# Fourier units between the halves of the output-gate units, folded weights cast one granule later, and a respaced folding stage in a one-core inference step

## The chip, the core and the metric

The kernel runs on one core of a Trainium2 chip. The metric is the time of the whole program in microseconds (us). Five engines work beside each other, each through its own list of instructions in order: TensorE (PE, the matmuls), VectorE (DVE), ScalarE (ACT), GpSimd (POOL) and SyncE (SP, which here only issues DMAs). Engines wait for each other through semaphores.

## The reference

One layer of a hybrid model on 384 tokens (128 context, 256 latent), model width 2048. The layer has a mixing sub-layer and a dense SwiGLU feed-forward; in each the input is normalised and modulated by six vectors of a per-layer map of the conditioning ("ada": `mod = silu(cond) @ w_ada + b_ada`). The change lies in the mixing sub-layer:

```python
proj = h @ w_in                       # GLA q, k, v, output gate g, decay factors, Fourier channels fo
o_f, s_f = gla_chunked(qh, kh, vh, la_f, s0_f, n_chunks)      # forward scan, la = log decay
o_b, s_b = gla_chunked(flip(qh), flip(kh), flip(vh), flip(la_b), s0_b, n_chunks)
o = rmsnorm_per_head(o_f + flip(o_b)) * gla_out_norm * silu(g)
f = fft2(fo.reshape(b, t, 4, 256), axes=(1, 3), norm='ortho').real
g_a, g_b = split(sigmoid(h @ w_gate + b_gate), 2)
merged = g_a * (o @ w_br_gla) + g_b * (f @ w_br_four)
return merged @ w_out, s_f, s_b
```

All values are float32.

## The kernel before

**Products in two parts.** Activations and weights are split into a rounded part (hi) and a remainder (lo), and a product is three matmuls: hi·hi, lo·hi, hi·lo. A weight granule is 128 x 1024 floats. SP loads it into `raw` (two buffers, in one stage up to two more); ACT casts it to `whi`; DVE subtracts to give `wlo`. `srcs` (from line 159) is the hand-written list of all granules in the order of use; `load` takes the next, `split` makes hi and lo, and `grab` returns the oldest finished pair and pushes one more through `load` and `split`. So each granule that PE begins to use emits, on SP, ACT and DVE, the work for granules that come later. `proj` is a product with the full 2048 rows: two granules, 24 matmuls each, into one PSUM tile `pmm`; what follows it (`dst`) is put in `later` and emitted after the first half of the next `proj`, or by `catch_up`.

**Order.** The order of instructions on PE, ACT, DVE and POOL is that of the code (a manual schedule); there is no planner. Side work is written as generators that are advanced one step per half of a `proj`; `paced` advances one by `rate[0]` steps a turn.

**Stages that the change touches.**

- GLA. Six q/k units and then 25 of the 32 gate units `h @ w_gate` run as `proj`, with the GLA heads as a side generator. Beside them a generator `ada` forms second-stage ada products: per step, POOL loads 512 KB of `w_ada` (`adaw`) and DVE adds it, weighted, to `adacc` (`ada_rest`, two instructions per step, 16 steps to a product), and at the end PE sums it over partitions with `selr` into `pr`; `ada_tail` copies this to `adev` (ACT), transposes it (`ptm`, PE) and writes `mods` (DVE). A gate unit ends on ACT with `gz` and a store of `gz` to DRAM (`gates_d`, line 962, by SP). In a head, ACT turns `z` into log decays `la` (lines 797 to 799), DVE makes the remainder `lal`, PE sums them to `bT`, and from this DVE makes `qi` and `ki`, with which PE forms `at` (line 854).
- Folding stage. The last seven gate units (14 half-units, "turns") run with `run_after` as their side work. Following the list `after` (lines 165 to 173) it folds h over mirrored positions, a pair of 128-row blocks at a time (`ends`: `t`, `r`; `over_parts`: `hF`), and multiplies the folded h by folded Fourier weights (`across_n`, eight steps for each of two halves of the channels, PSUM tiles `pfo`). The granules of `across_n` are unfolded in place by DVE (`fold_across`, lines 248 and 249). Here `raw` has two further buffers in another pool, named `raw3` in the order below.
- Output-gate stage (`mix_order`): eight units "o", each a `proj` of 48 matmuls ended by `gcol` (three transposes `pt`, the silu `gs` on ACT, `o_hi`), and after them Fourier units "b". `four` multiplies the spectrum by one granule of `w_br_four`, which `fold` first turns by DVE into sums and differences (`ws`, one buffer), copies out of PSUM (`fd`, ACT), assembles `y`, scales it by a gate (`gate`, sigmoid on ACT) and stores `y` to `four_d` in DRAM. Twelve of the sixteen "b" follow the "o" units 2 to 7, two each. A granule marked `hold` keeps its cast back until the unit's end (`settle`).
- The sixteen units "a" (`w_br_gla`) with the other four "b", then `w_out`. Another ada product, `summed` (`ada_gemv`), is formed on PE from `adaw` directly (`pr<-adaw,spad`) beside the "o" units.

```python
for b, i in mix_order:
    if b == "o":
        ...
        proj(psm, hT, lambda p, i=i: gcol(p, i), sd)
```

## Time and profile before

| | us |
|---|---|
| median of 3 runs | 1974.54 (1974.36 to 1977.55) |
| profiled execution, its own time | 1976.35 |
| its span in the trace | 1974.5 |
| PE busy | 1935.3 (98%) |
| DVE busy | 1637.8 (83%) |
| ACT busy | 914.5 (46%) |
| mean granted PE clock | 0.994 |

The stages in the trace, in us from the span's start: first modulation with the v and x products to about 145, GLA to 446, folding stage to 551, output-gate stage to 683, "a" units to 763, `w_out` to 905, a norm, and from 925 the feed-forward, whose order is the same in both kernels. A wait is an idle stretch of an engine put down to the instruction that released it; PE waits little, so each of its waits can be found by its place in these stages.

### The profile page before, as it was taken

How to read it: one execution, taken by the hardware profiler on the slowest of the kernel's cores; microseconds unless marked ns; L12 is line 12 of the kernel's file. 1: busy time of each engine (PE TensorE's matmuls, PEld its weight loads, DVE VectorE, ACT ScalarE, POOL GpSimd, SP SyncE). 2: the span in 40 equal slices, each digit the busy share in tenths (PEclk: the TensorE clock that was granted, in tenths of full speed). 3: DMA queues.
4: the chain of work that ended last, by engine and by line, in shares of the span. 5: the costliest groups of instructions: out<-in, count | busy, mean ns of one | idle time of the engine just before them, and what ended most of it. 6: DMA issues, size and time to landing. Idle time of an engine off the chain costs nothing.

```text
span 1974.5 us, 27637 instructions
## 1 busy us (share of the span) xinstructions
PE 1935.3 (98%) x10566; PEld 1699.0 (86%) x10566; DVE 1637.8 (83%) x2160; ACT 914.5 (46%) x1298; POOL 85.7 (4%) x154
## 2 busy tenths in 40 slices
PE   8998999999999899999999999999999999999997
PEld 5778999999988799999988888888888888888886
DVE  5668898888847688987789998999898989887885
ACT  4234445543555544446454444354444444444444
POOL 0000111110000000004000000000000000000001
PEclk9999999999999999999999999999999999999999
DMA  9976666775657787665335444453636263625243
GB/s 390 384 264 206 237 223 235 244 238 188 193 160 233 251 253 261 213 213 191 129 132 184 146 146 156 159 185 119 194 126 205 99 214 106 205 68 192 79 170 114
DMA packets 200616, 380.54 MB, mean 193 GB/s; under 512 B 14196, under 2 KB 126932, under 8 KB 196132
## 3 DMA queue, kind: packets, MB, share of 16 engines
q1 hardware_dynamic: 186004, 328.12, 48.9%
q0 software_dynamic: 13952, 50.39, 8.3%
q8 instruction: 83, 1.36, 0.3%
q14 instruction: 49, 0.40, 0.1%
q10 hardware_dynamic: 528, 0.26, 0.0%
HBM read 361.94 MB, written 16.78 MB: 192 GB/s over the span
## 4 chain that ended last, share of the span: by engine, by line
PE 80%; DVE 9%; DMA 5%; ACT 3%; issue 3%; SPq 0%; POOL 0%; DVEq 0%; ACTq 0%; POOLq 0%
PE pgu L327 30%; PE pmm L315 21%; PE pdn L327 17%; PE pv L477 3%; DVE adacc L679 2%; DVE wlo L276 1%; DMA raw<-in_w_in 1%; PE pgm L460 1%; PE pmm L1468 1%; PE pf L1205 1%; PE pfo L1017 1%; DMA slab<-in_w_ada 1%; PE ptr L1760 1%; DMA xraw<-in_w_x 1%; ACT whi L275 0%
## 5 line engine op out<-in xcount | busy, mean ns | idle before, releaser
L315 PE MATMUL pmm<-A_hi,whi 128*128 128x384 f32 x1072 | 364.9, 340 | 3.8 <-ACT gs L1167 3.8
L315 PE MATMUL pmm<-A_lo,whi 128*128 128x384 f32 x1072 | 360.9, 337 | 0.0
L315 PE MATMUL pmm<-A_hi,wlo 128*128 128x384 f32 x1072 | 360.4, 336 | 0.0
L1615 ACT CAST whi<-u 128x1024 fp32r<-128x1024 f32 x200 | 210.7, 1054 | 284.1 <-DVE u L1599 86.8
L1615 ACT CAST whi<-raw 128x1024 fp32r<-128x1024 f32 x175 | 184.1, 1052 | 197.8 <-PE pgu L327 59.9
L1626 DVE TENSOR_TENSOR wlo<-u,whi 128x1024 fp32r<-128x1024 f32 x200 | 244.5, 1222 | 32.9 <-ACT whi L1615 18.1
L275 ACT CAST whi<-raw 128x1024 fp32r<-128x1024 f32 x165 | 172.8, 1050 | 193.3 <-DMA raw<-in_w_gate 49.5
L276 DVE TENSOR_TENSOR wlo<-raw,whi 128x1024 fp32r<-128x1024 f32 x163 | 198.8, 1222 | 67.1 <-ACT whi L275 64.1
L327 PE MATMUL pgu<-whi,A_hi 128*128 128x512 f32 x640 | 250.1, 391 | 0.0
L327 PE MATMUL pgu<-whi,A_lo 128*128 128x512 f32 x640 | 249.3, 390 | 0.0
L1626 DVE TENSOR_TENSOR wlo<-raw,whi 128x1024 fp32r<-128x1024 f32 x175 | 213.8, 1222 | 36.0 <-ACT whi L1615 24.8
L315 PEld LDWEIGHTS pmm<-A_hi,whi 128*128 128x128 f32 x1072 | 202.8, 189 | 9.9 <-issue 4.5
L315 PEld LDWEIGHTS pmm<-A_lo,whi 128*128 128x128 f32 x1072 | 203.1, 189 | 0.6 <-DVE A_lo L365 0.5
L315 PEld LDWEIGHTS pmm<-A_hi,wlo 128*128 128x128 f32 x1072 | 202.8, 189 | 0.0
L679 DVE SCALAR_TENSOR_TENSOR adacc<-adaw,spad,adacc 128x1024 f32<-128x1024 f32 x150 | 185.8, 1281 | 1.6 <-DMA adaw<-in_w_ada 1.3
L327 PE MATMUL pdn<-whi,hid_hi 128*128 128x512 f32 x480 | 186.9, 389 | 0.0
L327 PE MATMUL pdn<-whi,hid_lo 128*128 128x512 f32 x480 | 186.8, 389 | 0.0
L327 PE MATMUL pgu<-wlo,A_hi 128*128 128x512 f32 x640 | 184.2, 389 | 0.0
L327 PEld LDWEIGHTS pgu<-whi,A_hi 128*128 128x128 f32 x640 | 120.2, 188 | 26.0 <-issue 0.8
L327 PEld LDWEIGHTS pgu<-wlo,A_hi 128*128 128x128 f32 x640 | 120.2, 188 | 25.3
L327 PEld LDWEIGHTS pgu<-whi,A_lo 128*128 128x128 f32 x640 | 120.2, 188 | 25.0
L327 PE MATMUL pgu<-whi,S 128*128 128x512 f32 x480 | 131.1, 395 | 0.0
(405 smaller groups left out, 3038.0 us busy)
## 6 DMA issues: line engine op xcount, KB each, us to landing
adaw<-in_w_ada POOLq DMA_DIRECT2D x96, 512.0 KB, 4.0
raw<-in_w_d SPq DMA_DIRECT2D x88, 512.0 KB, 3.8
slab<-in_w_ada SPq DMA_DIRECT2D x32, 1024.0 KB, 10.8
raw<-in_w_gate SPq DMA_DIRECT2D x64, 512.0 KB, 4.5
raw<-in_w_g SPq DMA_DIRECT2D x48, 512.0 KB, 3.3
raw<-in_w_u SPq DMA_DIRECT2D x48, 512.0 KB, 3.5
raw<-in_w_in SPq DMA_DIRECT2D x44, 512.0 KB, 4.3
u<-in_w_u SPq DMA_DIRECT2D x40, 512.0 KB, 4.6
```

The source lines that it names most:

```text
L275: ACT.copy(hi, raw)
L276: sub = lambda: eng.tensor_sub(lo, raw, hi.bitcast(F32))
L315: PE.matmul(dst, w[wi][:, k * n + n0 : k * n + n0 + P], x[xi][:, k0 + k, :], start=first and k == 0 and j == 0, stop=last and k == kts - 1 ...
L327: PE.matmul(dst, stat[x_][m], mov(w[w_], m), start=first and w_ == m == x_ == 0, stop=last and w_ == m == 1,)
L460: PE.matmul(pgv[q : q + 32, :], spad[:, k, :], slab[k // (KT // 2)][:, k % (KT // 2), :], start=k < 4, stop=k >= KT - 4,)
L477: PE.matmul(pv[2 * t + g], hT[x_][:, kb, t * P : (t + 1) * P], w_[:, g * 512 : (g + 1) * 512], start=kb == 0 and j == 0, stop=kb == KT - 1 ...
L679: DVE.scalar_tensor_tensor(acc[:, c, :], w, spad[:, k, c : c + 1], acc[:, c, :], op0=ALU.mult, op1=ALU.add,)
L1017: PE.matmul(p, w_of[0][:, i, k, g, :], x[:, :, lo:hi], start=kt == 0, stop=False)
L1205: PE.matmul(pf[:, 0 : 2 * HT], w[0][:, c], x[k], start=k == 0, stop=False)
L1468: PE.matmul(hp[u], hw[u][j][:, ((k - 1) % 8) * P : ((k - 1) % 8 + 1) * P], h2[m][:, k - 1, :], start=k == 1 and j == m == 0, stop=k == KT ...
L1615: ACT.copy(hi, src)
L1626: DVE.tensor_sub(lo, src, hi.bitcast(F32))
```

## The change

- Between the halves of the output-gate units 3 to 7 stands one Fourier unit, and one follows each of them; unit 2 is followed by one, and unit 7 by a second. `proj` gets `mid` for this. A unit in between with an odd number puts both of its PSUM tiles into the pool `pss`.
- The cast and the remainder of a folded granule are emitted at the next `split`, ahead of that granule's own; `hold` and `settle` are gone.
- `y` is kept in `unstored` and its store emitted a unit later.
- `summed` is advanced at the "a" units 0 and 3 (before 0 and 1), `ada` also at the "a" unit 5 and at turn 7 of the folding stage.
- Folding stage: the pairs get a free turn after the first four, the first `across_n` comes three turns after its `ends` (before two), and the second half of `across_n` goes into the last three turns.
- The last four steps of the fifth and last product of `ada_rest` run on PE (four matmuls each) in place of DVE; they fall among the half-units of `w_out`.
- `rate[0]` is 0.7 for the q/k units after the first (before 1.0), and 0.9 from `w_out` on (before 0.82).
- Gate units store `gz` from ACT's queue in place of SP's.

```diff
     for n in range(8):
-        after[n].append(("ends", n))
-        after[n + 1].insert(0, ("parts", n))
-        after[n + 2].insert(0, ("f", 0, n))
+        at = n + n // 4
+        after[at].append(("ends", n))
+        after[at + 1].insert(0, ("parts", n))
+        after[at + 3].insert(0, ("f", 0, n))
     for n in range(8):
-        after[10 + n * (turns - 10) // 8].append(("f", 1, n))
+        after[turns - 1 - (7 - n + 1) // 4].append(("f", 1, n))
...
-    mix_order = [("o", 0), ("o", 1)]
-    for i in range(2, 8):
-        mix_order += [("o", i)] + [("b", next(fourier)) for _ in range(BF * (i - 1) // 6 - BF * (i - 2) // 6)]
+    mix_order = []
+    between = [[] for _ in range(8)]
+    for i in range(8):
+        mix_order.append(("o", i))
+        if i > 2:
+            between[i].append(next(fourier))
+            mix_order.append(("b", between[i][0]))
+        mix_order += [("b", next(fourier)) for _ in range((i > 1) + (i == 7))]
...
         elif b == "b":
-            folded.add(len(srcs))
-            srcs.append(a["w_br_four"][i])
+            inner = any(i in x for x in between)
+            folded.add(len(srcs) - inner)
+            srcs.insert(len(srcs) - inner, a["w_br_four"][i])
...
+            for cast, _ in folded_due:
+                cast()
+            while folded_due:
+                folded_due.pop()[1]()
             if pairs == 1:
                 raw = fold(raw)
...
-            elif pairs and hold:
-                half_done.append(rest)
+            elif pairs:
+                folded_due.append((lambda: ACT.copy(hi, raw), low))
...
             step(side)
+            if not g:
+                for unit in mid:
+                    unit()
...
+            summed, pr = KT - 4 if (m, half) == todo[-1] else KT, None
             for k in range(KT):
                 w = adap.tile([P, 1024], F32, tag="adaw", name="adaw", bufs=2)
                 POOL.dma_start(w, a["w_ada"][m - 2, half, k])
+                if k >= summed:
...
+                    for j in range(4):
+                        PE.matmul(
+                            pr[32 * j : 32 * j + 32, :], spad[:, k, :], w[:, j * 256 : (j + 1) * 256],
+                            start=k == summed, stop=False,
+                        )
+                    yield
+                    continue
...
+        rate[0] = 0.7
         for i in qk_order[1:]:
             proj(psm, hT, keep(qk, i), sd)
+        rate[0] = 1.0
...
-                SP.dma_start(gates_d[i], g)
+                ACT.dma_start(gates_d[i], g)
...
-                if at == turns - 1:
+                if at in (7, turns - 1):
                     next(ada, None)
...
-            w = grab(hold=True)
             catch_up()
+            w = grab()
+            while unstored:
+                unstored.pop()()
...
-                pf = (pss if m else psm).tile([P, 512], F32, tag="side" if m else "mm", name="pf")
+                apart = m or i % 2
+                pf = (pss if apart else psm).tile([P, 512], F32, tag="side" if apart else "mm", name="pf")
...
-            SP.dma_start(four_d[i], y)
-            settle()
+            unstored.append(lambda: SP.dma_start(four_d[i], y))
+            gate_of()
...
-                proj(psm, hT, lambda p, i=i: gcol(p, i), sd)
+                proj(psm, hT, lambda p, i=i: gcol(p, i), sd, [lambda n=n: four(n) for n in between[i]])
...
-                if i < 2:
+                if i in (0, 3):
                     next(summed, None)
-                if KT - 7 <= i < KT - 2:
+                if i == 5 or KT - 7 <= i < KT - 2:
                     next(ada, None)
...
-        rate[0] = 0.82
+        rate[0] = 0.9
```

Where instructions stand now is shown at three places, before and then after; line numbers are those of each kernel. First ACT in the output-gate stage, one "o" unit with its two Fourier units. `gs` is the silu, `whi<-ws` the cast of folded Fourier weights, `whi<-raw` that of a granule of an "o" unit, `fd` the copy out of a Fourier unit's PSUM. Before:

```order
L1167 ACT_TABLE_LOAD
L1167 ACTIVATE gs<-pmm 128x384
L364 CAST o_hi<-gs 128x384
L1209 COPY fd<-pf 128x194 x2
L1192 ACT_TABLE_LOAD
L1192 ACTIVATE gate<-gate 128x384
L1209 COPY fd<-pf 128x194 x2
L275 CAST whi<-ws 128x1024
L1192 ACTIVATE gate<-gate 128x384
L275 CAST whi<-ws 128x1024
L275 CAST whi<-raw 128x1024 x2
```

After:

```order
L1194 ACT_TABLE_LOAD
L1194 ACTIVATE gs<-pmm 128x384
L376 CAST o_hi<-gs 128x384
L292 CAST whi<-ws 128x1024
L298 CAST whi<-raw 128x1024
L1239 COPY fd<-pf 128x194 x2
L1219 ACT_TABLE_LOAD
L1219 ACTIVATE gate<-gate 128x384
L292 CAST whi<-ws 128x1024
L298 CAST whi<-raw 128x1024
L1239 COPY fd<-pf 128x194 x2
L1219 ACTIVATE gate<-gate 128x384
```

The two casts of "o" granules, which stood together at the unit's end ahead of the next silu, stand apart, each behind the cast of a folded granule and ahead of a Fourier unit's copies.

Next DVE at the start of the folding stage. `raw3` with a fold (`128x2x256`) is the first granule of `across_n`; `hF` is what its matmuls read. Before:

```order
L248 TENSOR_TENSOR raw3_4518<-raw3_4518 128x2x256
L249 SCALAR_TENSOR_TENSOR raw3_4518<-raw3_4518 128x2x256
L709 TENSOR_TENSOR t_4556<-A_hi_92,A_lo_93 128x768
L714 TENSOR_TENSOR r_4557<-t_4556 128x2x64
L715 TENSOR_TENSOR r_4557<-t_4556 128x2x63
L714 TENSOR_TENSOR r_4557<-t_4556 128x2x128
L715 TENSOR_TENSOR r_4557<-t_4556 128x2x127
L282 TENSOR_TENSOR wlo_4530<-raw3_4518,whi_4529 128x1024
L276 TENSOR_TENSOR wlo_4569<-raw3_4520,whi_4568 128x1024
L721 TENSOR_TENSOR hF_4513<-r_4557,hF_4513 128x2x384
```

After:

```order
L285 TENSOR_TENSOR wlo_4511<-raw3_4502,whi_4510 128x1024
L734 TENSOR_TENSOR t_4538<-A_hi_92,A_lo_93 128x768
L739 TENSOR_TENSOR r_4539<-t_4538 128x2x64
L740 TENSOR_TENSOR r_4539<-t_4538 128x2x63
L739 TENSOR_TENSOR r_4539<-t_4538 128x2x128
L740 TENSOR_TENSOR r_4539<-t_4538 128x2x127
L254 TENSOR_TENSOR raw3_4504<-raw3_4504 128x2x256
L255 SCALAR_TENSOR_TENSOR raw3_4504<-raw3_4504 128x2x256
L746 TENSOR_TENSOR hF_4497<-r_4539,hF_4497 128x2x384
L734 TENSOR_TENSOR t_4580<-A_hi_92,A_lo_93 128x768
```

The gate granule now comes ahead of the first granule of `across_n` and goes first into the additional buffers; the first `hF` stands ahead of the remainder of the `across_n` weights.

Last ACT in a GLA head beside a gate unit. Before:

```order
L961 ACTIVATE gz<-pmm,bgate 128x384
L797 ACTIVATE la<-z 128x512
L797 ACTIVATE la<-z 128x256
L798 ACTIVATE la<-la 128x768
L799 ACT_TABLE_LOAD
L799 ACTIVATE la<-la 128x768
L364 CAST lah<-la 128x768
```

After:

```order
L988 ACTIVATE gz<-pmm,bgate 128x384
L989 DMA gates_d<-gz 128x384
L822 ACTIVATE la<-z 128x512
L822 ACTIVATE la<-z 128x256
L823 ACTIVATE la<-la 128x768
L824 ACT_TABLE_LOAD
L824 ACTIVATE la<-la 128x768
L376 CAST lah<-la 128x768
```

The store's issue stands between `gz` and the head's first step.

More of the change, by code (lines that the diff above doesn't have):

```diff
@@ L39 @@
 GF = 25
-BF = 12
 GD = 256
@@ L254, in fold_across, with split @@
         )
-    def split(at=None, eng=DVE, hold=False, defer=None):
+    def split(at=None, eng=DVE, defer=None):
         if raws:
@@ L270, in split, with low @@
             )
+            for cast, _ in folded_due:
+                cast()
+            while folded_due:
+                folded_due.pop()[1]()
             if pairs == 1:
                 raw = fold(raw)
[L274 to L277 removed]
+            def low():
+                eng.tensor_sub(lo, raw, hi.bitcast(F32))
                 ready.append((hi, lo))
@@ L281, in split, with push @@
                 ACT.copy(hi, raw)
-                low_due.append(lambda: (DVE.tensor_sub(lo, raw, hi.bitcast(F32)), ready.append((hi, lo))))
-            elif pairs and hold:
-                half_done.append(rest)
-            else:
-                rest()
-    def settle():
-        if half_done:
-            half_done.pop()()
-    def push(at=None, eng=DVE, hold=False):
+                low_due.append(low)
+            elif pairs:
+                folded_due.append((lambda: ACT.copy(hi, raw), low))
+            elif defer is not None:
+                ACT.copy(hi, raw)
+                defer.append(lambda: eng.tensor_sub(lo, raw, hi.bitcast(F32)))
+                ready.append((hi, lo))
+            else:
+                ACT.copy(hi, raw)
+                low()
+    def push():
         if not depth[0]:
@@ L683, in ada_rest @@
             yield
-            pr = pss.tile([P, 256], F32, tag="side", name="pr")
+            opened = pr is not None
+            if not opened:
+                pr = pss.tile([P, 256], F32, tag="side", name="pr")
             for c in range(2):
@@ L688, in ada_rest @@
                         pr[32 * j : 32 * j + 32, :], selr[:, 32 * c : 32 * c + 32],
-                        acc[:, c, j * 256 : (j + 1) * 256], start=c == 0, stop=c == 1,
+                        acc[:, c, j * 256 : (j + 1) * 256], start=c == 0 and not opened, stop=c == 1,
                     )
@@ L1232, in tile_step @@
             if b == "b":
-                for g in (df, nw):
-                    for _ in g:
-                        pass
-                four(i)
+                if not i:
+                    for g in (df, nw):
+                        for _ in g:
+                            pass
+                if not any(i in x for x in between):
+                    four(i)
             else:
```

25 lines of the change are left out of this document (13 added, 12 removed).

## The prediction, made before the changed kernel ran

> **What bounds the kernel now.** First the page, to see which engine is full; then TensorE's (PE's) waits, because a full engine loses time only where it waits; then stretches of equal work and the timeline, to see what each wait costs.
>
> ```profile
> span 1974.5 us, 27637 instructions
> PE 1935.3 (98%) x10566; PEld 1699.0 (86%) x10566; DVE 1637.8 (83%) x2160; ACT 914.5 (46%) x1298; POOL 85.7 (4%) x154
> ```
>
> PE is busy for 98% of the span. An edit that leaves PE's matmuls alone can only win back PE's waits and the slow clock behind them. PE's waits, longest in total first (us, times, longest):
>
> ```profile
> PE pmm L315 <- ACT gs L1167: 5.8, 4, 2.3
> PE at L854 <- DVE ki L831: 4.6, 1, 4.6
> ...
> PE pfo L1017 <- DVE hF L721: 4.2, 1, 4.2
> PE ptm L657 <- ACT adev L653: 2.8, 2, 2.3
> ...
> PE pr L687 <- DVE adacc L679: 1.1, 2, 0.6
> ...
> PE bT L814 <- DVE lal L365: 0.7, 1, 0.7
> ```
>
> All of these lie where the change works. What a wait drags behind it is read from the granted clock of the 3.5 us after five of them (start and end of a stretch, its length, busy time of PE, PEld, DVE, ACT and POOL with their instructions, then the clock, the DMA share and GB/s):
>
> ```profile
> 689.60:693.00 3.40, 3.40 (x12) 3.40 (x13) 3.37 (x7) 1.30 (x2) 0.00 (x0) 0.54 0.84 286
> 682.85:686.30 3.45, 3.45 (x20) 3.45 (x21) 2.80 (x9) 2.79 (x6) 0.00 (x0) 1.00 0.94 344
> 463.10:466.60 3.50, 3.50 (x16) 3.50 (x17) 3.43 (x8) 1.29 (x4) 0.00 (x0) 0.63 0.64 208
> 648.00:651.50 3.50, 3.50 (x14) 3.50 (x13) 2.86 (x10) 3.16 (x7) 0.00 (x0) 0.55 0.54 150
> 877.40:880.90 3.50, 3.50 (x13) 3.50 (x13) 2.98 (x8) 0.33 (x1) 0.00 (x0) 0.57 0.96 327
> ```
>
> Behind the 2.3 (ptm) the clock was 0.54, behind the 4.2 (pfo) 0.63, behind the 2.3 (pmm at 647.68) 0.55, behind the three short ones at 874 to 877 0.57; behind the pmm wait that ended at 682.85 it stayed 1.00. (At full clock 20 matmuls took 3.45: 0.17 each.) So such a stretch costs 3.4 x 0.46 = 1.6, 3.5 x 0.37 = 1.3, 3.5 x 0.45 = 1.6 and 3.5 x 0.43 = 1.5 us more.
>
> **The change part by part.**
>
> *Fourier units between the halves.* Four stretches of the output-gate stage, from one unit's wait to the next; each holds one output-gate unit and two Fourier units, in the same columns:
>
> ```profile
> 614.45:629.50 15.05, 15.05 (x103) 13.64 (x101) 11.16 (x23) 8.07 (x11) 1.05 (x2) 1.00 0.74 253
> 629.50:647.68 18.18, 15.42 (x103) 13.72 (x101) 12.15 (x26) 10.05 (x16) 1.05 (x2) 1.00 0.67 220
> 647.68:665.51 17.83, 16.82 (x101) 15.26 (x101) 12.12 (x25) 9.49 (x14) 1.06 (x2) 0.90 0.71 222
> 665.51:682.85 17.34, 15.28 (x101) 13.72 (x101) 12.12 (x25) 9.49 (x14) 1.05 (x2) 1.00 0.76 247
> ```
>
> The first had no wait and took 15.05 for the same matmuls. Why the others wait is on the timeline:
>
> ```profile
> 639.41 0.33 SPq L227 DMA_DIRECT2D raw<-in_w_in  x1
> 644.78 1.05 ACT L275 CAST whi<-raw 128x1024 fp32r<-128x1024 f32 x1 [3.31 <-DMA raw<-in_w_in]
> 647.14 0.49 ACT L1167 ACTIVATE gs<-pmm 128x384 f32<-128x384 f32 x1
> 647.68 0.44 PE L315 MATMUL pmm<-A_hi,whi 128*128 128x384 f32 x1 [2.28 <-ACT gs L1167]
> ```
>
> ACT stands in order. A cast whose weights were still in flight (issued 639.41, cast 644.78: 5.37) stood ahead of the silu (with its table load between, from the cast's end at 645.83 to 647.14), and the silu frees the PSUM tile that PE's next unit writes. The change puts a Fourier unit between the two halves, so that the silu of the last unit now stands ahead of these casts on ACT, and the folded cast is emitted at the next granule's split. PE's matmuls per unit are as many as before; DVE has 12.15 and ACT 10.05 of work for 15.05 of PE, so neither is full. With every unit at 15.05: 18.18 + 17.83 + 17.34 - 3 x 15.05 = **-8.2**. The other end is -5, if one unit in three keeps its wait. I take -8.2, since a unit of that length stands in the trace. The y stores, a unit later on SP, stand behind weight loads that are needed sooner; the first reader is an "a" unit several units on: nothing.
>
> *summed.* The tail of the second-stage ada product was: copy at the first "a" unit, transposes at the next, PE waiting 2.3 for the copy. The transposes now come three units later, when the copy has long run: -2.3 and the slow stretch of 1.6, **-3.9** (to -2.3 if the stretch comes back elsewhere).
>
> *Folding stage.* Rows from its start:
>
> ```profile
> 451.73 0.38 SPq L227 DMA_DIRECT2D raw<-in_w_in  x1
> 455.48 0.69 DVE L248 TENSOR_TENSOR raw<-raw 128x512 f32<-128x512 f32 x1 [4.13 <-DMA raw<-in_w_in]
> 456.82 0.95 DVE L709 TENSOR_TENSOR t<-A_hi,A_lo 128x768 f32<-128x768 f32 x1
> 458.88 1.22 DVE L282 TENSOR_TENSOR wlo<-raw,whi 128x1024 fp32r<-128x1024 f32 x1
> 463.11 0.42 PE L1017 MATMUL pfo<-hF,whi 128*128 128x388 f32 x1 [4.20 <-DVE hF L721]
> ```
>
> PE came to its first across unit at 463.11 - 4.20 = 458.91 and waited for DVE, which had waited 4.13 for a load that could go only at 451.73. Now one more half gate unit lies ahead, 24 matmuls of 0.17, 4.1: PE comes at 463.0. DVE now runs, from the landing near 455.5: cast and remainder of the gate granule (1.05 + 1.22), one fold of a pair up to its remainder step (458.88 - 456.82 = 2.06), the unfolding of the weights (456.82 - 455.48 = 1.34), hF (0.95), another 2.06 and the remainder of the across weights (1.22): 455.5 + 9.9 = 465.4, less some overlap of neighbouring instructions (0.1 each, about 0.4). So 465.0, and with PE coming between 463.0 and 463.1 the wait is about 1.9 in place of 4.2, -2.3; and as the wait before 682.85, 17.34 - 15.28 = 2.06, left the clock whole, the slow 1.3 goes as well: **-3.6**. Bounds: -5.5 (both all gone) and -1 (the bunched across units of the last turns wait for weights).
>
> *Fewer ada steps at the start (rate 0.7).*
>
> ```profile
> 178.89 3.86 SPq L227 DMA_DIRECT2D raw<-in_w_in  x2
> 184.74 1.05 ACT L275 CAST whi<-raw 128x1024 fp32r<-128x1024 f32 x1 [8.12 <-DMA raw<-in_w_in]
> 193.94 0.59 PE L854 MATMUL at<-qi,ki 128*64 128x64 f32 x12 [4.57 <-DVE ki L831]
> ...
> raw<-in_w_in SPq DMA_DIRECT2D x44, 512.0 KB, 4.3
> ```
>
> Two ada steps of DVE fewer stand ahead of ki, but the chain to it starts at a cast that waited for a DMA, not for DVE. That load, the first of the pair issued from 178.89 on, took 5.8 where such loads land in 4.3 (median); with two fewer 512 KB ada loads beside it I give it 4.3: **-1.4**. Bounds: 0 (it stays 5.8) and -5.9 (the wait of 4.57 gone with its slow clock). The 0.9 in w_out meets no wait of PE there: nothing.
>
> *Last ada product partly on PE.*
>
> ```profile
> 603.45 0.34 PE L315 MATMUL pmm<-A_hi,wlo 128*128 128x384 f32 x1
> 603.72 0.64 PE L700 MATMUL pr<-adaw,spad 128*32 128x256 f32 x8
> 604.57 0.34 PE L315 MATMUL pmm<-A_lo,whi 128*128 128x384 f32 x1
> 876.84 0.56 PE L657 MATMUL ptm<-ident,adev 128*128 128x128 f32 x2 [0.49 <-ACT adev L653]
> ```
>
> Four steps move from DVE to PE. One such step between matmuls takes 604.57 - 603.45 - 2 x 0.17 = 0.78, so four cost **+3.1**. In return the two waits for adacc go (**-1.1**), and with them I take half of the slow 1.5 (**-0.8**): the 0.49 for adev stays.
>
> *Gate stores on ACT.* A store now stands on ACT between gz and la:
>
> ```profile
> 244.94 0.57 ACT L961 ACTIVATE gz<-pmm,bgate 128x384 f32<-128x384 f32 x1
> 245.41 0.86 ACT L797 ACTIVATE la<-z 128x512 f32<-128x512 f32 x2
> 251.33 0.96 DVE L365 TENSOR_TENSOR lal<-la,lah 128x768 fp32r<-128x768 f32 x1 [0.96 <-ACT lah L364]
> 252.70 0.27 PE L814 MATMUL bT<-cg,lal 128*128 128x128 f32 x1
> 1965.71 0.42 ACTq L1916 DMA_DIRECT2D out_yT<-x1b  x1
> gates_d<-gz SPq DMA_DIRECT2D x32, 192.0 KB, 3.7
> ```
>
> It waits for gz's end (245.51) and takes 0.42 (ACT's only other DMA kind), so la starts about 0.65 later. lal ended 0.4 ahead of bT here, and in another head PE already waited 0.7 for it: 0.25 + 0.65 + about 0.1 for the three heads that have such a chain, **+1.0** (0 to +2.1). The other stores lie beside an ACT that is busy 46%. The Trainium skill's page "DMA: Bandwidth & Descriptors", section "Issuing engines are not separate DMA queues", says that issuing from a second engine saves only the issuing sequencer's time; by that the move wins nothing but SP's issue, and no term here counts a gain for it.
>
> Sum: -8.2 - 3.9 - 3.6 - 1.4 + 3.1 - 1.1 - 0.8 + 1.0 = **-14.9**. The profiled execution took 1976.35, span 1974.5; it would take 1961.4. The median is 1974.54: forecast **1959.6**.
>
> **The rivals.**
>
> *Only the waits of the mixing stage go.* The folding stage and the start keep theirs, since both begin with a load that starts no sooner. -8.2 - 3.9 - 1.9 + 3.1 + 1.0 = -9.9: 1964.6. For it: both chains start at a DMA. Against: the folding stage gets 4.2 of PE work ahead of the wait.
>
> *The slow clock is not the waits' doing.* The Trainium skill's page "TensorE: Matmul & The Clock Gate", section "Part 1: The HAM clock gate", ties half speed to an idle window of about 3.4 us, free-running; the trace disagrees, with 0.54 and 0.55 behind waits of 2.3. As a mechanism of this kernel: if those stretches come by their own rhythm, the 1.6 of ptm, the 1.6 in the mixing stage and the 0.8 stay, +4.0: 1963.6.
>
> *ACT is held until its store lands.* Were it held for the 3.7 of the store's row, la would start 3.8 later in three heads: 3.4 + 3.8 + 3.4 = 10.6, each with a slow stretch of about 1.5, less the 1.0 counted: +14.1, so 1973.7. It decides once ACT's delay passes 0.65 by far. Against: the row of 0.42 is the issue alone.
>
> *Two raw buffers bound each Fourier unit (slower).* A unit of four granules over two raw buffers takes two rounds of load to cast 5.37, cast 1.05, remainder 1.22 and what its steps stand in a queue. With no queueing that is 15.3, hardly over the 15.05. If the folded cast, a granule later, puts two steps of about 0.95 more into each round, 1.9, a unit is 2 x 9.54 = 19.1, and with a slow stretch of 1.5 it is 20.6. The stage has about four such units of (15.05 + 18.18 + 17.83 + 17.34) / 4 = 17.1: +14 in place of -8.2, 1981.8. It turns slower once a unit passes some 19 us. For it: three of four stretches were 17.3 to 18.2, and their wait began at a load. Against: one ran at 15.05 on the same two buffers, and the late cast was read from ws, a buffer of its own.
>
> **How the numbers follow.** Forecast 0.60, waits of the mixing stage alone 0.15, clock rhythm 0.05, ACT held 0.08, two buffers 0.12. A measurement of this kernel can tell about 0.2%, 3.9 us, so faster is below 1970.6 and slower above 1978.5: faster 0.60 + 0.15 + 0.05 = 0.80, same 0.08, slower 0.12. The range leaves out the last two: its high end, 1969, has the bounds at -5 for the units, -2.3 for summed, 0 at the start and little in the folding stage; its low end, 1951, has the waits at the start and in the folding stage gone (-4.5 and -1.9 more) and the store free.
>
> **What would show it.** In the profile after: no wait of pmm for gs, stretches of about 15 us per output-gate unit at clock 1.00; no ptm wait near 690; a pfo wait of about 2 near 465; at waiting about 3 near 192; no wait for adacc near 875; bT waiting in two or three heads for under 1. A cast waiting for raw in the Fourier units, with PE waiting for wlo or whi behind it, would make the forecast wrong; so would la following its store by 3 us or more.

## The result, and the profile after

The changed kernel takes 1977.63 us (median of 19 runs, 1975.27 to 1981.23), the kernel before 1974.11 (19 runs): ratio 1.0022, 95% interval [1.0015, 1.0029]. It is slower by about 0.2%, where 0.8% faster was forecast. Its profiled execution took 1977.9, 1.5 over the 1976.35 of before. The medians stand 3.5 apart, so the profiles below account for the 1.5 only.

The top of the page after: PE is as full as before.

```profile
span 1976.0 us, 27636 instructions
...
PE 1937.8 (98%) x10598; PEld 1698.8 (86%) x10598; DVE 1628.8 (82%) x2152; ACT 916.4 (46%) x1298; POOL 86.1 (4%) x154
```

PE's waits after (us in total, times, longest): the four waits of pmm for gs are gone. Those of pfo, the across units of the folding stage, come six times and add up to 7.6 (before three times and 4.7). And pmm now waits for gate, a DVE step of the a units.

```profile
PE at L879 <- DVE ki L856: 4.8, 2, 4.6
...
PE pfo L1045 <- DVE wlo L285: 3.7, 3, 2.3
PE pmm L324 <- DVE gate L1285: 3.3, 2, 2.8
PE pfo L1044 <- ACT whi L289: 3.2, 2, 2.4
...
PE z L814 <- ACT krs L802: 1.7, 1, 1.7
PE ptm L669 <- ACT adev L665: 1.0, 1, 1.0
PE pfo L1044 <- DVE X L1052: 0.7, 1, 0.7
```

`X` is the sum of the first channel half, which DVE adds up from pfo before PE can write the second half into it.

The stages tell more than the waits. These are stretches of the same work, cut at landmarks on PE: folding stage (last po to first pfq), output-gate stage (first pt to first matmul on o), a units to the last Fourier unit, the six a units behind it, w_out (which after holds the last ada product's matmuls too, 838 for 806). Columns as in the prediction. Before:

```profile
437.79:548.63 110.84, 106.17 (x644) 105.07 (x642) 92.00 (x135) 50.57 (x84) 5.32 (x10) 0.98 0.60 190
569.65:682.85 113.20, 107.37 (x705) 95.60 (x703) 74.10 (x143) 61.20 (x93) 7.39 (x14) 0.98 0.67 214
682.85:738.35 55.50, 53.20 (x309) 52.88 (x310) 48.69 (x93) 30.18 (x53) 0.53 (x1) 0.97 0.83 262
738.35:763.27 24.92, 24.92 (x145) 24.92 (x145) 22.80 (x32) 8.82 (x15) 2.11 (x4) 1.00 0.93 331
763.27:903.67 140.40, 138.69 (x806) 135.78 (x806) 119.44 (x147) 65.44 (x105) 8.44 (x16) 0.99 0.61 205
```

After:

```profile
437.87:555.26 117.39, 109.76 (x643) 107.74 (x641) 94.27 (x137) 51.46 (x84) 5.94 (x11) 0.96 0.60 189
576.27:681.23 104.96, 104.96 (x705) 94.12 (x704) 74.71 (x144) 61.86 (x97) 7.42 (x14) 1.00 0.70 224
681.23:733.48 52.25, 51.70 (x311) 51.44 (x310) 45.76 (x90) 26.55 (x46) 0.53 (x1) 1.00 0.86 285
733.48:763.54 30.06, 26.79 (x146) 26.20 (x145) 27.45 (x37) 11.61 (x20) 2.65 (x5) 0.94 0.88 305
763.54:904.97 141.43, 139.77 (x838) 134.86 (x838) 113.94 (x142) 64.65 (x104) 9.54 (x18) 1.00 0.62 210
```

Folding stage +6.55, output-gate stage -8.24, first a units -3.25, last a units +5.14, w_out +1.03; with the GLA end at 437.87 against 437.79 (+0.08) that is the +1.3 which PE is late at the end of w_out. In this pair of profiles 11.5 us were won in the middle and 12.7 lost around it.

### The profile page after: what moved, and what is told of

It reads as the page before. It is cut to its first block, busy times and chain, and to the rows that moved or that the text cites. A ratio compares the mean times of both kernels' runs of the same rounds, so it can differ in the third digit from the quotient of the medians.

```text
span 1976.0 us, 27636 instructions
## 1 busy us (share of the span) xinstructions
PE 1937.8 (98%) x10598; PEld 1698.8 (86%) x10598; DVE 1628.8 (82%) x2152; ACT 916.4 (46%) x1298; POOL 86.1 (4%) x154
## 4 chain that ended last, share of the span: by engine, by line
PE 64%; DVE 7%; DMA 2%; ACT 2%; issue 2%; ACTq 0%; DVEq 0%; POOLq 0%
PE pgu L336 30%; PE pdn L336 17%; PE pmm L324 11%; DVE wlo L285 1%; DMA raw<-in_w_br_gla 1%; DVE adacc L702 1%; PE pmm L1504 1%; ACT whi L298 1%; PE pf L1235 1%; PE pfo L1044 1%; PE ptr L1796 1%; DMA raw<-in_w_d 0%; PE pr L725 0%; ACT whi L289 0%; DVE t L734 0%
## 5 line engine op out<-in xcount | busy, mean ns | idle before, releaser
L1651 ACT CAST whi<-raw 128x1024 fp32r<-128x1024 f32 x175 | 184.4, 1054 | 199.1 <-PE pgu L336 56.6
L298 ACT CAST whi<-raw 128x1024 fp32r<-128x1024 f32 x149 | 156.2, 1051 | 176.1 <-DMA raw<-in_w_out 49.3
L702 DVE SCALAR_TENSOR_TENSOR adacc<-adaw,spad,adacc 128x1024 f32<-128x1024 f32 x142 | 175.9, 1281 | 4.2 <-DMA adaw<-in_w_ada 3.9
```

The costliest lines, as they stand in the source:

```text
L298: ACT.copy(hi, raw)
L702: DVE.scalar_tensor_tensor(acc[:, c, :], w, spad[:, k, c : c + 1], acc[:, c, :], op0=ALU.mult, op1=ALU.add,)
L1651: ACT.copy(hi, src)
```

## The experiments

Every group ran beside the kernel before, which had medians of 1973.1 to 1973.7 in them. The experiments' medians are of 5 to 12 runs; a difference of two kernels under 2 us is not told apart here. Each has one profile, which can lie up to 4 us off its median.

**Undoing parts of the changed kernel.** The folding stage of before, without the ada step at turn 7:

```diff
-        at = n + n // 4
-        after[at].append(("ends", n))
-        after[at + 1].insert(0, ("parts", n))
-        after[at + 3].insert(0, ("f", 0, n))
+        after[n].append(("ends", n))
+        after[n + 1].insert(0, ("parts", n))
+        after[n + 2].insert(0, ("f", 0, n))
...
-                if at in (7, turns - 1):
+                if at == turns - 1:
```

> The changed kernel with the folding stage as before: the old list of pairs and across units, and no ada step at turn 7. In the profiles of before and after PE is 6.6 us later at the end of that stage. Theory A (respacing and the ada step together cost it): the stage ends 6.6 us earlier than in the changed kernel, but the tail of the a units, where the changed kernel lost 5.1 us while loads were late, may take part of it: 1977.6 - 6.6 = 1971.0 if nothing is given back, 1974 to 1976 if the a units give back half or more. Rival (the stage is late because the gate stores go from ACT's queue or because of the earlier lower ada rate): no change, 1977.6, and the across units still wait over 3 us in the second half of the stage.

1973.46, ratio to the kernel before 0.9995 [0.9986, 1.0004]: 4.2 less than the changed kernel. The stage took 112.70 in place of 117.39:

```profile
437.38:550.08 112.70, 107.16 (x644) 105.45 (x642) 91.97 (x135) 50.91 (x84) 5.32 (x10) 0.97 0.58 188
```

The loss is in the respacing or the step. Without the step alone (only the last two lines of that diff):

> The changed kernel without the ada step at turn 7 alone. Theory A1 (the step of 2.48 us on DVE stands ahead of the unfolding of across weights, PE waits 2.4 + 0.6 for them at 506 to 508 and runs at half clock behind it): these two waits are gone, the folding stage is about 4.5 us shorter, 1973 to 1975 in all if the a units don't take it back. Rival A2 (the spacing itself, with across units bunched in the last turns): the waits at 506 stay or move by a turn, the stage is shorter by less than 1.5 us, total above 1976.

1976.78, ratio 1.0014 [1.0002, 1.0026]. The stage still took 116.70; the wait of 2.4 shrank to 0.8, but another of 0.8 and one of 2.0 for X stood behind it. A1 fell and A2 held: it is mostly the spacing.

The last four steps of the fifth ada product on DVE again:

```diff
-            summed, pr = KT - 4 if (m, half) == todo[-1] else KT, None
+            summed, pr = KT, None
```

> The changed kernel with the last four steps of the fifth ada product on DVE again. By the prediction's terms (+3.1 for the matmuls on PE, -1.1 for the two waits on adacc, -0.8 for the slow clock) this gives 1.2 us back: 1976.4, with two waits for adacc of 0.6 near the end of w_out. Rival (DVE's earlier end in w_out is worth more than the sums show, or these matmuls lie in PE's shadow): no gain, or slower by 1 to 2 us.

1974.86, ratio 1.0002 [0.9993, 1.0011]: 2.8 less, more than the 1.2 by the prediction's terms. Both undone together:

> The changed kernel with the folding stage of before (old list, no ada step at turn 7) and the fifth ada product all on DVE: the two edits of the first experiments that gave time back, together. If they add (4.2 and 2.8 by the medians of the first experiments): 1977.6 - 7.0 = 1970.6, some 3 under the kernel before. If the a units or the w_out stage take it back, since PE then meets their loads earlier: 1973 or more.

1973.52, ratio 0.9991 [0.9981, 1.0001]. They do not add: the second case held. In its profile waits stand elsewhere, with 30.53 for the last a units and 2.6 for adacc at the end of w_out.

**The output-gate stage alone.** The kernel before with only `mix_order`, `mid`, `folded_due` and `unstored` of the change:

> The kernel before with only the output-gate stage changed: Fourier units between the halves, folded casts a granule later, y stored a unit later. By the trace of the changed kernel that stage alone is 8.2 us shorter (first pt to first matmul on o: 113.3 before, 105.0 after). Theory (the a units behind it are paced by loads, with the DMA engines at a share of 0.97, and so give back what PE gains beyond about 3): the stage is 8.2 shorter, the stretch from the last Fourier unit to the last a unit grows from 24.9 to 27 or more, and the total is 1974 - 8.2 + 2 to 5 = 1968 to 1971. Rival (all of the gain stays): 1965.9. Other rival (the gain of that stage needs the other edits): 1973 and the stage over 110.

1965.89, ratio 0.9957 [0.9941, 0.9972]: 7.6 us faster than before. Run again in a later group:

> The same kernel as m0_mix_only, run beside the three others as their base: 1966 to 1968.5, the stretch from the last Fourier unit to the last a unit 25 to 26.5, no wait for ki over 4.6.

1965.65, ratio 0.9964 [0.9952, 0.9976]. The stages of the second run:

```profile
439.21:550.30 111.09, 106.18 (x643) 105.08 (x641) 91.94 (x135) 50.57 (x84) 5.33 (x10) 0.98 0.61 189
571.33:676.29 104.96, 104.96 (x705) 94.13 (x704) 73.13 (x143) 59.72 (x94) 7.41 (x14) 1.00 0.68 222
676.29:728.76 52.47, 51.94 (x312) 51.42 (x310) 45.49 (x89) 29.48 (x51) 0.00 (x0) 1.00 0.85 281
728.76:755.60 26.84, 25.16 (x145) 24.87 (x145) 25.48 (x35) 9.48 (x16) 2.58 (x5) 1.00 0.92 331
755.60:894.30 138.70, 137.02 (x806) 134.22 (x806) 119.80 (x148) 66.00 (x105) 8.55 (x17) 1.00 0.61 208
```

The output-gate stage is at 104.96 as in the changed kernel, PE without one wait in it. The rival held in the total, as nearly all of the stage's gain reaches the end; the theory's give-back of 2 to 5 was too dark. This kernel is the base of what follows: the changed kernel is 12 us above it, and all of that is the other edits. To the base each of them was added alone.

**Ada step at the a unit 5.**

```diff
-                if KT - 7 <= i < KT - 2:
+                if i == 5 or KT - 7 <= i < KT - 2:
```

> The kernel with only the output-gate stage changed (1965.9), and besides only the ada step at the a unit 5. Theory V (a units with an ada step need 5.1 us of DVE for 4.2 of PE, so the five steps at the units 9 to 13 live on the lead of the weights, and one more step of 2.48 takes that lead): the stretch from the last Fourier unit to the last a unit grows from 25.7 to about 29, and since the step is no longer needed in w_out about 1 comes back there: 1967.5 to 1970. Rival (the loss in that stretch comes from the other edits): within 1 of 1965.9, stretch under 26.5.

1969.20, ratio 0.9976 [0.9964, 0.9988]: 3.4 over the base, the last a units at 27.16 and not at 29 (base 26.84 and, in the first run, 25.67). So it costs, but its place in the profile isn't shown.

**New folding stage and its step.**

> The kernel with only the output-gate stage changed (1965.9), and besides only the new folding stage (list and ada step at turn 7). Theory (DVE has 6.6 us of work for a pair's turn of 6.5 on PE, so what starts later there ends later; the list leaves DVE idle in one turn and the step adds 2.48): first across unit to the weights' own first matmul after the stage (first pfo to first pfq) 91 to 93 in place of 86 to 87, total 1965.9 + 4 to 6 = 1970 to 1972. Rival (the loss needs the stores on ACT or the lower ada rate): under 1968.

1971.22, ratio 0.9993 [0.9984, 1.0002]: 5.4 over the base, the stage at 115.97 against 111.09. The theory holds: the loss comes without the other edits. DVE in the folding stage shows how. From its first step there to the end of the eighth pair's (before, then after):

```profile
455.48:512.49 57.01, 52.34 (x310) 51.41 (x309) 52.80 (x81) 26.92 (x44) 1.49 (x4) 0.97 0.57 185
456.89:518.46 61.57, 54.66 (x300) 53.04 (x299) 53.71 (x80) 26.23 (x42) 0.82 (x3) 0.92 0.54 172
```

Before, DVE works 52.80 of 57.01 us, so it needs nearly all of a pair's turn. After, it has hardly more to do (53.71) and takes 4.6 longer: most of that is idle time. Its steps in the changed kernel (the groups left out are steps of the same turns):

```profile
456.89 1.22 DVE L285 TENSOR_TENSOR wlo<-raw,whi 128x1024 fp32r<-128x1024 f32 x1 [5.08 <-ACT whi L298]
...
491.96 1.23 DVE L285 TENSOR_TENSOR wlo<-raw,whi 128x1024 fp32r<-128x1024 f32 x1 [1.91 <-ACT whi L298]
...
503.44 2.48 DVE L702 SCALAR_TENSOR_TENSOR adacc<-adaw,spad,adacc 128x1024 f32<-128x1024 f32 x2
505.82 0.69 DVE L254 TENSOR_TENSOR raw<-raw 128x512 f32<-128x512 f32 x1
...
508.41 1.22 DVE L285 TENSOR_TENSOR wlo<-raw,whi 128x1024 fp32r<-128x1024 f32 x1 [0.30 <-ACT whi L289]
```

DVE begins 1.4 later than before (456.89 against 455.48). It idles 1.91 just behind the free turn, waiting for ACT's cast of a gate granule, and has the ada step of 2.48 just ahead of the unfolding that PE waits for (2.4 and 0.6, up to 508.43 and 509.69). Behind the first wait, of 2.31 up to 465.63, the clock stays whole; behind the next four it falls (after, same columns as the stages):

```profile
463.00:467.83 4.83, 2.52 (x18) 2.20 (x16) 4.03 (x8) 2.46 (x4) 0.00 (x0) 1.00 0.37 102
467.83:471.00 3.17, 3.17 (x20) 3.17 (x19) 3.14 (x7) 0.61 (x2) 0.00 (x0) 1.00 0.94 269
...
474.50:478.00 3.50, 3.50 (x15) 3.50 (x16) 3.46 (x7) 0.69 (x2) 0.00 (x0) 0.53 0.65 187
508.40:511.00 2.60, 1.99 (x6) 1.59 (x7) 1.83 (x2) 1.51 (x2) 0.00 (x0) 0.51 0.63 240
```

The half clock, added up over the stage from the clock's records, costs 5.1 us (before 1.7). With the 3.0 more of waits this makes 6.4 of the 6.55.

**Only the across units a turn later**, without the free turn, the bunching or the step (and with the rate 0.9 in w_out, for which the kernel with that rate alone, below, is the base):

```diff
-        after[n + 2].insert(0, ("f", 0, n))
+        after[n + 3].insert(0, ("f", 0, n))
...
-        rate[0] = 0.82
+        rate[0] = 0.9
```

> The kernel with only the output-gate stage changed, the rate 0.9 in w_out, and the first eight across units one turn later, without the free turn, the bunching and the ada step of the changed kernel. Theory (only the first wait of the stage is to be had, since DVE needs all of each pair's turn): the first wait falls from 4.4 to about 2 and DVE isn't set back otherwise, from the last po to the first pfq 109 to 110 in place of 111.0, 1 to 2 less than b1. Rival (DVE's later start of 1.4 with the gate granule first is carried through all eight pairs): waits of 0.8 at each following pair, 0 to 2 more than b1.

1966.46, ratio 0.9967 [0.9956, 0.9978], 3.6 over its base. The rival held in kind: the first wait fell to 2.1, six more for wlo (0.2 to 0.5, under the 0.8 expected) and one of 1.5 for X came, and the stage took 112.79 against 111.28. Where the other 2 of the 3.6 lie isn't shown. So a turn's delay costs 1.5 of the 4.9 that the stage lost with the whole list and the step.

```profile
PE pfo L1030 <- DVE wlo L285: 3.8, 7, 2.1
PE pfo L1029 <- DVE X L1037: 1.5, 1, 1.5
```

**Gate stores on ACT.**

```diff
-                SP.dma_start(gates_d[i], g)
+                ACT.dma_start(gates_d[i], g)
```

> The kernel with only the output-gate stage changed (1965.9), and besides only the gate stores on ACT's queue. By the prediction's term (la 0.65 later in three heads, +1.0): 1966.9, with 1 to 3 us of waits of bT. Rival (ACT held till the store lands): +13, 1979; the traces of the changed kernel speak against it, la follows its store within 0.5. Rival (no cost, as bT has no wait in the changed kernel): 1965.9 within 0.5.

1968.64, ratio 0.9983 [0.9973, 0.9992]: 2.9 over the base. ACT in a head of this kernel:

```profile
244.01 0.57 ACT L973 ACTIVATE gz<-pmm,bgate 128x384 f32<-128x384 f32 x1
244.61 0.33 ACTq L974 DMA_DIRECT2D gates_d<-gz  x1
244.99 0.87 ACT L809 ACTIVATE la<-z 128x512 f32<-128x512 f32 x2 [0.40 <-ACT gz L973]
```

From gz to la it is 0.98, before 0.47: 0.5 later, and ACT is not held for the landing. bT waits 1.6 in this profile, and 0.9 and 1.9 in the two of the base, so it shows no cost there. The profiled run, 1965.93, was the fastest of the eleven: where the 2.9 lies isn't shown.

**Last four steps on PE.**

> The kernel with only the output-gate stage changed (1965.9), and besides only the last four steps of the fifth ada product on PE. Here DVE isn't late at the end of w_out (waits of 0.66, 0.47 and 0.49 there), so the four groups of matmuls cost 3.1 and give back the two waits on adacc (1.1) and perhaps the slow clock behind them (1.5): 1966.4 to 1968. Rival (they hide): 1965 or less.

1969.02, ratio 0.9981 [0.9968, 0.9993]: 3.2 over the base, w_out at 142.35 against 138.70. The cost of 3.1 holds about; what it was to give back isn't there, as a wait of 1.0 for adev and one of 0.7 for a load of adaw stand where those for adacc were.

**The ada rate.** 0.7 in the five q/k units alone, and with 0.9 in w_out:

```diff
+        rate[0] = 0.7
         for i in qk_order[1:]:
             proj(psm, hT, keep(qk, i), sd)
+        rate[0] = 1.0
```

> The kernel with only the output-gate stage changed, and besides only the ada rate 0.7 in the five later q/k units. Theory W (two or three ada steps fewer at the start put every later step two or three places back, so that the five steps in the a units are all full DVE steps of 2.48, where some were the gap and the tail between two products, and the last product ends late in w_out): the stretch from the last Fourier unit to the last a unit grows from 25.7 by 2 to 4, PE waits 2 or more for adacc before 875, total 3 to 6 over the repeat of the base kernel in this group; up to 1.5 comes back at the start if the first wait for ki is shorter. Rival (rate has no effect, the loss of the full kernel comes from the edits acting together): within 1 of the base.

> As the one before, and with the rate 0.9 in w_out. Theory W: the faster rate there takes back the wait for adacc near the end of w_out (2 or so) but not what the a units lose: 1.5 to 4 over the base. Rival (the faster rate makes DVE late for the weights of w_out): as slow as with 0.7 alone or slower, with waits of pmm for wlo or whi in w_out.

1980.10, ratio 1.0035 [1.0023, 1.0047], 14 over the base; and 1973.95, ratio 1.0004 [0.9996, 1.0013], 8 over it. This is the costliest edit by itself, and both theories had less (3 to 6, 1.5 to 4). The longest of PE's waits, and DVE at the end of w_out, with 0.7 alone:

```profile
PE pr L699 <- DVE adacc L691: 12.5, 1, 12.5
```

```profile
869.75 4.86 DVE L691 SCALAR_TENSOR_TENSOR adacc<-adaw,spad,adacc 128x1024 f32<-128x1024 f32 x4
876.40 2.48 DVE L691 SCALAR_TENSOR_TENSOR adacc<-adaw,spad,adacc 128x1024 f32<-128x1024 f32 x2 [1.78 <-DMA adaw<-in_w_ada]
```

PE sums adacc at a fixed place near the end of w_out, and DVE was still making it. Counted in the traces, DVE's adacc instructions (two to a step) by stage are, GLA / folding to output gate / a units / w_out: base 108 / 6 / 10 / 36; with 0.7 100 / 6 / 10 / 44; changed kernel 100 / 8 / 12 / 32, and the four steps on PE. The rate takes four steps out of GLA. The changed kernel makes them up by one step at turn 7, one at the a unit 5 and two more in w_out, where four go on PE and DVE has two fewer. With the rate 0.9 besides, the wait for adacc was still 8.3 in three parts. The theory had the cause of this wait and not its size; the last six a units took 26.80 with 0.7 alone, within the base's 25.67 to 26.84, so there it was wrong.

0.9 in w_out alone:

> The kernel with only the output-gate stage changed (1965.7 and 1965.9), and besides only the ada rate 0.9 in place of 0.82 in w_out. Theory W (the last ada product must be summed at a fixed place near the end of w_out, and what DVE has not done by then PE waits for): the waits of 0.5 for adacc and 0.5 for adev at 867 to 869 get shorter and the slow clock behind them goes, 1 to 2.5 less: 1963.5 to 1965. Rival (the faster rate makes DVE late for w_out's weights): slower than 1966.5.

1962.88, ratio 0.9949 [0.9937, 0.9960]: 10 us under the kernel before, 2.8 under the base, and the fastest kernel of the study. The theory holds: w_out takes 137.53, with no wait for adacc or adev.

```profile
727.32:752.25 24.93, 24.93 (x145) 24.91 (x145) 23.87 (x33) 9.47 (x16) 2.61 (x5) 1.00 0.95 343
752.25:889.78 137.53, 136.90 (x807) 134.37 (x807) 119.64 (x148) 66.04 (x105) 8.48 (x17) 1.00 0.63 210
```

The changed kernel with only the rate back at 1.0:

> The whole changed kernel with only the ada rate at the start back at 1.0. Theory W (the rate 0.7 puts off four ada steps, which the steps at turn 7 and at the a unit 5, the rate 0.9 and the four steps on PE then do at places where they cost PE time): with the debt gone but the places where it was paid still there, the a units lose less (stretch from the last Fourier unit to the last a unit 26 to 28 in place of 30.1), 2 to 4 less: 1973.5 to 1975.5; what is left over the base is the folding stage (5 to 6) and the matmuls on PE. Rival (the payment alone costs it, whatever the rate): within 1 of 1977.6.

1980.25, ratio 1.0036 [1.0023, 1.0050]: 2.6 more, where both theories had the same or less. In its profile GLA ended at 444.52 in place of 437.87:

```profile
PE bT L839 <- ACT lah L376: 2.0, 1, 2.0
...
PE bT L839 <- DVE lal L377: 0.7, 1, 0.7
```

(That profile was the slowest of six runs, so its 6.7 is more than the usual loss.) In the changed kernel bT has no wait. Nor has it in any of the nine profiles with the rate 0.7, of which two have the stores on SP; in the eleven with 1.0 it waits 0.5 to 2.7, whichever engine stores. So the lower rate takes these waits of the GLA heads away by itself. Whether the stores on ACT need it isn't shown.

**summed.** Its second step at the a unit 3 alone:

```diff
-                if i < 2:
+                if i in (0, 3):
```

> The kernel with only the output-gate stage changed, and besides only the second step of summed at the a unit 3 in place of 1. In the base there is no wait for adev any more, so by that nothing is left to gain: within 1 of the base. By the prediction's term (2.3 and a slow stretch of 1.6 saved by this edit) 3.9 less.

1967.11, ratio 0.9967 [0.9955, 0.9978]: the same as the base within the spread.

Added up, the edits cost 24 us one by one on the base (3.4, 5.4, 2.9, 3.2, 8.2 for both rates, 1.3) and 12 together. So they overlap or make up for each other, and no part's price alone is its share of the 12.

**The last a units.** Two kernels on top of the one with both parts undone, whose last a units took 30.53. First, the loads of the residual input in w_out:

```diff
+            if i in (0, 4, 8):
+                x1_load(i // 4 + 1, POOL)
             sq0 = add_sq(qs[0], p, i == 0)
```

> The first kernel of this group with three of the four loads of the residual input (786 KB each, needed only from the fifth unit of w_out on) issued in w_out by POOL in place of the a units. Theory D (in the a units the DMA engines are full, and these 2.4 MB, about 6.7 us at 350 GB/s, lie in the way of the weights): PE's waits for gate and whi from 685 to 765 are gone, the stretch from the last Fourier unit to the last a unit is back at 25.0 from about 27, 2 to 3 us less in all. Rival (the pace is DVE's, 95% busy there, or the buffers'): the waits stay within 0.5.

1976.62, ratio 1.0010 [1.0001, 1.0020]: slower in all by 3 (in w_out PE waits 4.3 for adacc, where it was 3.1, and 1.9 for `A_lo`), but the stretch fell to 26.80. Giving y two buffers of its own, the other way to free the stores, doesn't fit: the pool needs 29 kB a partition and 27.25 are left, so that kernel has no time. Then five buffers for y and yb:

> The first kernel of this group with five buffers in place of four for yb and y (and one in place of two for gz in the folding stage, to make room). Theory R (the load of yb for the thirteenth a unit waits until the last y store has landed, 7.6 us in the changed kernel, and holds the next weight load on SP): that load is issued some 5 us earlier and the stretch from the last Fourier unit to the last a unit is back at 25.0, 2 us or more less. Theory D (the DMA engines are full): earlier issue, as late a landing, less than 1 us.

1972.41, ratio 0.9992 [0.9983, 1.0001], 1.1 less and so not told apart. The load of yb went out 5.8 earlier, at 737.75 and not 743.58, as theory R had it; but the stretch was 27.39 and not 25.0, which is against that load being the limit. The three stretches, each row from its own kernel's profile, first that with both parts undone:

```profile
728.75:759.28 30.53, 26.97 (x145) 26.39 (x145) 28.02 (x39) 11.40 (x20) 2.65 (x5) 0.94 0.86 302
```

With the loads in w_out:

```profile
729.55:756.35 26.80, 25.53 (x146) 24.79 (x145) 26.60 (x36) 10.45 (x18) 3.10 (x6) 1.00 0.83 287
```

With five buffers:

```profile
729.42:756.81 27.39, 25.44 (x145) 24.86 (x145) 26.16 (x35) 9.81 (x18) 2.60 (x5) 1.00 0.88 324
```

In neither is there the single wait of 3 with the slow clock behind it. But that doesn't show what took it away: the kernel with the old folding stage alone, with neither edit, has 26.78. None gets back to 24.92, and in the second row DVE is busy for 26.60 of 26.80. A unit with an ada step takes DVE about 5.1, by the starts of its gate steps in the changed kernel:

```profile
744.68 0.55 DVE L1285 TENSOR_TENSOR gate<-gate,pmm 128x384 f32<-128x384 f32 x1
...
746.21 2.48 DVE L702 SCALAR_TENSOR_TENSOR adacc<-adaw,spad,adacc 128x1024 f32<-128x1024 f32 x2
749.04 1.22 DVE L285 TENSOR_TENSOR wlo<-raw,whi 128x1024 fp32r<-128x1024 f32 x1 [0.35 <-ACT whi L298]
750.18 0.55 DVE L1285 TENSOR_TENSOR gate<-gate,pmm 128x384 f32<-128x384 f32 x1
```

750.18 - 744.68 = 5.5, less the 0.35 of idle, 5.15, for the 24.92 / 6 = 4.15 of PE. By these numbers the five such units (9 to 13) use up a lead of five us, an estimate, and a DVE that comes to them late makes PE wait. The step at the a unit 5 stands ahead of this stretch, and the counts fit a DVE that it makes late: 9 or 10 adacc instructions fall into the stretch in the nine profiles with that step, 8 (once 9) in the ten others that have the new output-gate stage. The stretch took 26.6 to 30.5 in the nine and 24.9 to 29.5 in the ten; which run gets the long wait isn't settled by one profile each.

## Why the prediction was wrong

By its own steps, as profiled (forecast, then measured):

- *Fourier units between the halves*, -8.2, was -8.24, and alone -7.6 and -7.8 in the total. The waits for the silu are gone and no unit kept one: this step was right. Which of its edits (the units' place, the later cast, the later store of y) it takes was not told apart.
- *summed*, -3.9, was -3.25 in its stretch, but for another reason, and that is luck: in the base, with the steps at the a units 0 and 1 as before, that stretch also takes 52.47 in place of 55.50, and the shift alone gives nothing there. The copy `adev` stood on ACT behind a cast of folded weights (687.80, and the copy at 689.18); in the base it stands ahead of that cast.
- *Folding stage*, -3.6, was +6.55: the first step that failed. The first wait came out as worked (2.3 against 1.9), and the clock stayed whole behind it. The working stopped there: it priced the first wait and took DVE to catch up behind it. But DVE needs nearly all of a pair's turn (52.80 of 57.01 before), so what it begins later (1.4) or idles (1.91 at one place) comes out at later across units, as waits of 0.6 to 2.4 with the slow clock twice. The bound of -1 left 2.6 for later waits; they took 10.2 more than the forecast. The ada step at turn 7 is little of it: without it the stage is 0.7 shorter. How the rest parts between the free turn and the bunching is open.
- *Fewer ada steps*, -1.4 (its own rows give 5.85 - 4.3 = 1.5), was nothing: at waited 4.6 as before. The steps ahead of ki were about as counted: up to 195 us DVE did 12 adacc instructions in place of 17, two to a step. But the term didn't ask where the four steps that GLA loses go. With the old places they cost 8 to 14 in w_out; in the changed kernel they stand at turn 7, at the a unit 5 and on PE. "The 0.9 in w_out meets no wait: nothing" was wrong the other way, as it is worth 2.8 on the base.
- *Last ada product on PE*, +3.1 - 1.1 - 0.8: the 3.1 shows alone, at 142.35 against 138.70, and the 1.9 to come back doesn't: alone the edit costs 3.2, and taking it out of the changed kernel gives 2.8. That w_out as a whole came out at +1.03 is luck, since the rate 0.9 works there too.
- *Gate stores on ACT*, +1.0: la came 0.5 later, as worked (0.65). Alone the kernel is 2.9 slower, and the waits of bT don't show why.
- *Left out*: the last a units, +5.14. The prediction followed PE's 11 us to the last Fourier unit and did not ask what stands behind it. There a unit with an ada step takes DVE 5.1 for PE's 4.15, the DMA engines are busy 0.83 to 0.95 in the rows shown, and an extra ada step was put ahead. "Where a stall goes, what is late next" had to be asked at the end of the gain, too.

The low end of the range adds up to 1952 by its own terms and not to 1951; that changes nothing.

Of the rivals none was this. "Only the waits of the mixing stage go" came nearest, as the folding stage gained nothing, but had it stand still. Two raw buffers bounded nothing: the stage ran on them without a wait of PE. ACT was not held. Against the clock's own rhythm stands the output-gate stage: with the waits the slow clock went too, from 0.98 to 1.00.

## What to carry to other kernels

Keep a ledger of side work: when a rate or a list takes steps from one place, find the place that gets them, and price that. Before spacing work out on an engine, add up its work for a turn against the turn; where it is nearly full, what it begins late or idles at the start comes out at the end, whatever happens to the first wait. And test the parts of a bundle one by one: here one part was worth 8 us, and the others together cost 12, though one of them, the rate 0.9, is worth 2.8 by itself.

## What the runs showed of the hardware

A wait of PE of 2.30 was followed by a clock of 0.54 (before, at 689.59), and one of 2.31 by 1.00 (after, at 465.63), while two of 0.81 and 0.82 within 2 us were followed by 0.53. So the length of a wait alone doesn't say whether the slow stretch comes, and the prediction's reading of 2.06 as short enough was luck.

The clock's records show more than the rows by 3.5 us do. From 10 to 1969 us each slow stretch of these two profiles is 3.41 long at half clock, or twice that (after, from 508.48), so 3.41 of it cost 1.7 and not 1.3 to 1.6. And the starts stand a whole number of 3.41 apart: before they are at 194.35, 464.01, 648.32, 689.28 and 877.02, which is 79, 54, 12 and 55 times 3.41. On this grid the wait of 2.28 up to 647.68 lies whole in one window, and a slow one followed; the 2.31 up to 465.63 lies across a border (464.10), 0.78 and 1.53, and none did. The 0.81 and 0.82 share one window. How much waiting in a window it takes isn't settled: 1.63 was followed by a slow one (after, up to 474.34), 1.67 was not (before, up to 682.46).

The Trainium skill's page "TensorE: Matmul & The Clock Gate", section "Part 1: The HAM clock gate", speaks of a free-running window, which fits two outcomes for one length; its idle window of about 3.4 us does not fit, as none of these waits filled one.

The wait for ki at 190 was 4.1 to 4.6 in most profiles and 1.7 to 1.9 in four. The two profiles of one kernel, the output-gate stage alone, had 1.9 and 4.6. That is 2.7 us which come and go from run to run, as much as several of the edits are worth.
